# Attention: dividing the values' results instead of the probabilities, and moving the scores' scale and a sign onto the normalised queries

## The chip, the cores and the metric

The kernel runs on one core of one Trainium2 chip. The metric is the device time of one execution in microseconds (us), as the median of several runs; each version is also profiled once by the hardware profiler, and the rows in this document come from those profiles. PE is TensorE's matmul, PEld its weight load, DVE is VectorE, ACT is ScalarE, POOL is GpSimd and SP is SyncE.

## What is computed

The reference is a two-layer backbone of a diffusion generator: 512 latent tokens and 256 context tokens of width 1024. Each layer projects the normalised tokens into three groups of heads (attention, a state-space scan in both directions, and a Hyena long convolution), joins them in an output projection, and then applies a mixture of 16 experts. Only attention matters here:

```python
ql = apply_rope(rmsnorm(heads(q_l, ATT_HEADS), q_norm[i]), cos, sin)      # 6 query heads of 64
kl = apply_rope(rmsnorm(heads(k_l, ATT_KV_HEADS), k_norm[i]), cos, sin)   # 2 key and value heads
kc = rmsnorm(heads(k_c, ATT_KV_HEADS), k_norm[i])
att_l = gqa_blocks(ql, jnp.concatenate([kc, kl], axis=1), jnp.concatenate([vc, vl], axis=1))
att_c = gqa_blocks(qc, kc, vc)                 # in layer 0 only

def one_block(qi):                             # 128 queries at a time
    s = jnp.einsum('bqgrd,bkgd->bgrqk', qi, k).astype(jnp.float32) * scale    # scale = 1/8
    p = jax.nn.softmax(s, axis=-1).astype(v.dtype)
    return jnp.einsum('bgrqk,bkgd->bqgrd', p, v)
```

## The kernel before

Tokens lie in blocks of 128 (`P`): four latent blocks and two context blocks. Each layer first projects to queries, keys and values (`qkv`). `rotate` then normalises them: for each block it squares (L856) and sums (L857) each head's 64 values into `ss`, whose last axis holds six query heads and two key heads; L858 and L859 turn this into reciprocal roots, and L864 multiplies the heads by them. `to_heads` transposes queries and keys into `QT` and `KT`.

`attention` works through the six heads for one pair of query blocks at a time: blocks 0 and 1 against all six key blocks, blocks 2 and 3 against all six, and in layer 0 the two context blocks against the two context key blocks. That makes 18 calls of `values` in layer 0 and 12 in layer 1, and 60 calls of `scores`, one per head and query block. `scores` puts the products of a query block with all keys into a double PSUM bank of kind "A" (L920), takes the maximum over the keys (L923, VectorE) and multiplies it by -0.125 (L924, VectorE), takes the exponential on ScalarE with that as bias and 0.125 as scale, which also adds up the row's sum `su` (L927), and inverts the sum (L929, VectorE). GpSimd then multiplies the probabilities `pt` by it (L930). `values` runs one head later, so that the scores of the next head are under way. It goes through the key blocks two at a time, here called a round: TensorE transposes four 128x128 pieces of the probabilities into a PSUM bank (L939), VectorE or ScalarE copies them to `ph` (L942), and TensorE multiplies them with the values into the bank `po` (L945), the first query block on rows 0 to 63 and the second on rows 64 to 127. A call has three rounds for six key blocks and one round for two: 42 rounds in layer 0 and 36 in layer 1, 78 in all. Two ScalarE copies (L951) then bring the result into `mixa`.

Attention is a generator, and `weave` mixes its steps with other work. In layer 0 these are the last of the scan, then the Hyena convolutions (`hy_conv`, L517 on) and matmuls of the modulation (L256); in layer 1 projections, then scan (`ssd_states` and `ssd`, L670 on) and convolutions. The convolutions multiply spectra on VectorE (L551, L552, L554 to L556, L558) and on GpSimd (L550, L553, L557, L559); L540 adds a PSUM bank to an SBUF tile on VectorE. In the scan, GpSimd has L735, L740, L751, L774 and half of L717 and L718.

The order in which each engine gets its instructions is made ahead of time: the program is traced in the order of the code, and a scheduler with a simulated timeline (`schedule_with_timeline_sim=True`) places each instruction in its engine's queue. An engine then takes its queue in order. PSUM has eight banks; `B0` and `BA`, `B3` say how many each kind of use has. In layer 0's attention kind "A" has two double banks and kind "p" (`po` and the transposes) two banks. In layer 1, kind "A" has one double bank; "p" shares three banks with others (`BA`), and later has two of its own (`B3`).

## Time and profile before

| what | value |
|---|---|
| median of three runs | 1469.62 us (1465.35 to 1476.77) |
| the profiled execution: its time | 1466.34 us |
| the profiled execution: its span | 1464.4 us |
| mean granted TensorE clock | 0.925 of 2.4 GHz |
| instructions | 23682 |

The span is the time from the first to the last instruction; what lies around it is 1.9 us. A row of the trace that groups instructions gives the line of the code, the engine, the operation, the tile written and the tiles read, shapes and a count, then the busy time of the group, the mean duration of one in ns, and how long the engine stood idle just before them with what ended most of that. The granted clock is a share of full speed. It has two levels, 0.5 (1.2 GHz) and 1.0 (2.4 GHz), so 0.88 over a stretch says how long each was granted.

### The profile page before, as it was taken

What the parts mean: (1) busy time and instruction counts of PE and PEld (TensorE: products, weight loads), DVE (VectorE), ACT (ScalarE), POOL (GpSimd) and SP (SyncE); (2) the same over time, 40 slices, a digit from 0 to 9 for tenths busy, and PEclk for the clock granted to TensorE, in tenths of its full rate; (3) what the DMA queues carried; (4) which work ended last, traced back from release to release, by engine and by line L of the source; (5) the groups of instructions that cost most, each with busy time, mean ns of one, the idle gap of its engine ahead of it and who ended that gap; (6) DMA issues with size and microseconds to landing.
All of it is one profiled execution on the core that took longest, in us unless ns stands there. A gap on an engine that the chain in (4) does not pass through costs nothing. (4 is left out here: it accounts for less than half of the span.)

```text
span 1464.4 us, 23682 instructions
## 1 busy us (share of the span) xinstructions
PE 1248.4 (85%) x8904; PEld 899.8 (61%) x8904; DVE 760.8 (52%) x1661; ACT 488.4 (33%) x1056; POOL 453.9 (31%) x497
## 2 busy tenths in 40 slices
PE   5999999899899899869998949988988888599780
PEld 2787787677677677634544428876776776345440
DVE  6854652644667875852332334754498475512121
ACT  4332334445233453311110144444454542111111
POOL 3220321544334524222323311321188412222221
PEclk9999999997799999979998969999999899699995
DMA  7744536343655163279999551111301173999954
GB/s 295 241 157 158 173 102 215 118 152 132 206 161 184 58 244 117 86 275 369 340 322 279 110 173 44 58 58 44 138 30 58 41 288 129 352 371 353 354 115 137
DMA packets 88809, 265.04 MB, mean 181 GB/s; under 512 B 10397, under 2 KB 13101, under 8 KB 88048
## 3 DMA queue, kind: packets, MB, share of 16 engines
q1 hardware_dynamic: 76016, 224.39, 43.5%
q0 software_dynamic: 12672, 39.07, 10.4%
q8 instruction: 72, 1.18, 0.3%
q14 instruction: 49, 0.40, 0.1%
HBM read 231.62 MB, written 31.79 MB: 180 GB/s over the span
## 5 line engine op out<-in xcount | busy, mean ns | idle before, releaser
L1417 PE MATMUL bank<-we,xh 128*32 128x128 f32 (+3 forms) x1280 | 208.7, 394 | 12.1 <-DVE y L1473 8.6
L1417 PEld LDWEIGHTS bank<-we,xh 128*32 128x32 f32 (+3 forms) x1280 | 99.5, 139 | 106.1 <-issue 76.9
L219 PE MATMUL bank<-hh,hw 128*128 128x512 f32 (+1 forms) x440 | 159.5, 362 | 0.1
L220 PE MATMUL bank<-hl,hw 128*128 128x512 f32 (+1 forms) x440 | 157.1, 357 | 0.0
L221 PE MATMUL bank<-hh,lw 128*128 128x512 f32 (+1 forms) x440 | 156.7, 356 | 0.4 <-DVE lw L207 0.4
L1474 POOL DMA_INDIRECT xd<-y,txi x35 | 56.6, 1618 | 177.7 <-DMA xd<-y,txi 90.2
L1417 PE MATMUL bank<-we,gh 128*32 128x256 f32 (+3 forms) x392 | 101.0, 522 | 2.8 <-ACT gh L1450 1.4
L219 PEld LDWEIGHTS bank<-hh,hw 128*128 128x128 f32 x440 | 85.4, 194 | 12.1 <-issue 1.0
L221 PEld LDWEIGHTS bank<-hh,lw 128*128 128x128 f32 x440 | 84.6, 192 | 12.8 <-DVE lw L207 0.9
L220 PEld LDWEIGHTS bank<-hl,hw 128*128 128x128 f32 x440 | 85.0, 193 | 11.4 <-issue 0.8
L930 POOL TENSOR_SCALAR pt<-pt,su 128x768 f32<-128x768 f32 (+1 forms) x60 | 55.0, 924 | 118.6 <-DVE su L929 97.6
L256 PE MATMUL bank<-mraw,c 128*32 128x128 f32 x1536 | 72.8, 295 | 16.9 <-DMA mraw<-in_wm_dram 11.8
L1393 POOL DMA_INDIRECT xg<-hd,tk x40 | 40.4, 1009 | 96.6 <-PE bank L1407 32.7
L207 DVE TENSOR_TENSOR lw<-rw,hw 128x1024 fp32r<-128x1024 f32 (+1 forms) x36 | 44.7, 1243 | 49.1 <-ACT hw L206 48.9
L256 PEld LDWEIGHTS bank<-mraw,c 128*32 128x32 f32 x1536 | 41.2, 114 | 41.4 <-DMA mraw<-in_wm_dram 16.0
L945 PE MATMUL bank<-ph,vt 128*64 128x128 f32 x624 | 53.8, 292 | 15.1 <-DVE ph L942 7.0
L1417 PEld LDWEIGHTS bank<-we,gh 128*32 128x32 f32 (+3 forms) x392 | 35.7, 143 | 49.6 <-issue 41.8
L220 PE MATMUL bank<-lo,mh 128*128 128x512 f32 x160 | 63.8, 399 | 1.5 <-DVE lo L207 1.5
L219 PE MATMUL bank<-ho,mh 128*128 128x512 f32 x160 | 64.5, 405 | 0.4 <-ACT ho L206 0.4
L221 PE MATMUL bank<-ho,ml 128*128 128x512 f32 x160 | 63.2, 395 | 0.0
L206 ACT CAST hw<-rw 128x1024 fp32r<-128x1024 f32 (+1 forms) x36 | 37.8, 1049 | 76.1 <-PE bank L220 48.0
L923 DVE TENSOR_REDUCE mx<-banks 128x1 f32<-128x768 f32 (+1 forms) x60 | 50.3, 844 | 23.3 <-PE banks L920 23.1
(478 smaller groups left out, 2744.9 us busy)
## 6 DMA issues: line engine op xcount, KB each, us to landing
we<-in_we_dram SPq DMA_DIRECT2D x192, 512.0 KB, 11.3
mraw<-in_wm_dram SPq DMA_DIRECT2D x192, 256.0 KB, 3.6
rw<-in_wi_dram SPq DMA_DIRECT2D x34, 512.0 KB, 3.5
ro<-in_wo_dram SPq DMA_DIRECT2D x16, 512.0 KB, 4.9
G<-ar SPq DMA_DIRECT2D x10, 768.0 KB, 3.9
xd<-ox SPq DMA_DIRECT2D x10, 512.0 KB, 2.7
hd<-h POOLq DMA_DIRECT2D x10, 512.0 KB, 2.9
xf<-xd SPq DMA_DIRECT2D x10, 512.0 KB, 7.0
```

What stands on the lines that cost most here:

```text
L206: ACT.copy(hi, src)
L207: (lo_eng or DVE).tensor_sub(lo, src, f(hi))
L219: PE.matmul(o, lh, rh, start=start, stop=False)
L220: PE.matmul(o, lh, rl, start=False, stop=False)
L221: PE.matmul(o, ll, rh, start=False, stop=stop)
L256: PE.matmul(ps[32 * k:32 * k + 32, 0:P], c32[:, 4 * h + k, 30 - 2 * j:62 - 2 * j], raw[:, k], start=(j + h == 0), stop=(j == n - 1 and h = ...
L923: DVE.tensor_reduce(mx, ps, axis=AX.XY, op=OP.max)
L930: POOL.tensor_scalar(pt[:, 0:nkt * P], pt[:, 0:nkt * P], su, 1.0, OP.mult, OP.mult)
L945: PE.matmul(po[64 * q:64 * q + 64, 0:P], vt[:, k0 + kt + j, h // 3], ph[:, (2 * j + q) * P:(2 * j + q + 1) * P], start=(kt + j == 0), stop ...
L1393: POOL.indirect_dma_start(out=xg[0:c], out_offset=None, in_=hd, in_offset=bass.IndirectOffsetOnAxis(ap=R.token(i)[0:c], axis=0))
L1417: PE.matmul(ps[r:r + c, 0:m], lh[:, 0:c], w[:, m * j:m * j + m], start=start, stop=stop)
L1474: POOL.indirect_dma_start(out=xd.rearrange("t (n m) -> (t n) m", n=n), out_offset=bass.IndirectOffsetOnAxis(ap=R.row(i)[r], axis=0), in_=y ...
```

## The change

The queries' reciprocal roots are multiplied by -0.125 in `rotate`, so that a product of scores comes out as minus an eighth of what it was. The minimum over the keys is then the bias of the exponential as it stands, and the exponential's scale is -1. The probabilities stay undivided. `scores` returns the inverted sums beside them, and `su` has six buffers instead of four. In the first round of a call of `values`, two further matmuls, with the inverted sums repeated over 64 columns as the stationary operand and the identity as the moving one, spread the inverted sums of the two query blocks over the other 128 columns of the bank `po`, each over 64 rows. At the end ScalarE copies these columns to SBUF (`rb`, one copy of 128x128), and VectorE multiplies each half of the result by them while it brings it into `mixa`, in place of the two ScalarE copies.

```diff
@@ -857,6 +857,8 @@
             DVE.tensor_reduce(ss[:, t, h0:8], sq[:, h0:8], axis=AX.X, op=OP.add)
         ACT.activation(ss, ss, AF.Sqrt, bias=eps, scale=1.0 / HD)
         DVE.reciprocal(ss, ss)
+
+        DVE.tensor_scalar(ss[:, :, 0:6], ss[:, :, 0:6], -0.125, None, OP.mult)
         for t in range(TA):
             h0 = 0 if t < nq else 6
             nh = 8 - h0
@@ -920,15 +922,13 @@
                     PE.matmul(ps[:, j, 0:hw], QT[:, h, qs], KT[:, h // 3, x, ks], start=(x == 0), stop=(x == 1))
             ps = ps[:, 0:nb, 0:hw]
             mx = sm.tile([P, 1], F32, name="mx", bufs=4)
-            DVE.tensor_reduce(mx, ps, axis=AX.XY, op=OP.max)
-            DVE.tensor_scalar(mx, mx, -0.125, None, OP.mult)
+            DVE.tensor_reduce(mx, ps, axis=AX.XY, op=OP.min)
             pt = pool.tile([P, 768], F32, name="pt", bufs=PB[l])
-            su = sm.tile([P, 1], F32, name="su", bufs=4)
-            ACT.activation(pt[:, 0:nkt * P].rearrange("p (a b) -> p a b", a=nb), ps, AF.Exp, bias=mx, scale=0.125,
+            su = sm.tile([P, 1], F32, name="su", bufs=6)
+            ACT.activation(pt[:, 0:nkt * P].rearrange("p (a b) -> p a b", a=nb), ps, AF.Exp, bias=mx, scale=-1.0,
                            accum_out=su)
             DVE.reciprocal(su, su)
-            POOL.tensor_scalar(pt[:, 0:nkt * P], pt[:, 0:nkt * P], su, 1.0, OP.mult, OP.mult)
-            return pt
+            return pt, su
 
         def values(h, q0, k0, nkt, pts):
             po, busy["po"] = bank("p"), True
@@ -936,19 +936,27 @@
                 ps = bank("p")
                 for j in range(2):
                     for q in range(2):
-                        PE.transpose(ps[:, (2 * j + q) * P:(2 * j + q + 1) * P], pts[q][:, (kt + j) * P:(kt + j + 1) * P],
+                        PE.transpose(ps[:, (2 * j + q) * P:(2 * j + q + 1) * P], pts[q][0][:, (kt + j) * P:(kt + j + 1) * P],
                                      ident)
                 ph = pool.tile([P, 512], F32, name="ph", bufs=2)
                 (ACT.copy if kt % 4 else DVE.tensor_copy)(ph, ps)
+                if kt == 0:
+
+                    for q in range(2):
+                        PE.matmul(po[64 * q:64 * q + 64, P:2 * P], pts[q][1].to_broadcast([P, 64]), ident, start=True,
+                                  stop=True)
                 for j in range(2):
                     for q in range(2):
                         PE.matmul(po[64 * q:64 * q + 64, 0:P], vt[:, k0 + kt + j, h // 3],
                                   ph[:, (2 * j + q) * P:(2 * j + q + 1) * P], start=(kt + j == 0), stop=(kt + j == nkt - 1))
                 if kt == 2:
                     yield
+            rb = pool.tile([P, P], F32, name="rb", bufs=2)
+            ACT.copy(rb, po[:, P:2 * P])
             for q in range(2):
                 s = slice((q0 + q) * P, (q0 + q + 1) * P)
-                ACT.copy(mix[64 * (h % 2):64 * (h % 2) + 64, h // 2, s], po[64 * q:64 * q + 64, 0:P])
+                r = slice(64 * q, 64 * q + 64)
+                DVE.tensor_mul(mix[64 * (h % 2):64 * (h % 2) + 64, h // 2, s], po[r, 0:P], rb[r])
             busy["po"] = False
             yield
 
```

## Rows read from the trace of the kernel before

**Rows 1.** The page: each engine's busy time, share of the span, instructions.
```profile
PE 1248.4 (85%) x8904; PEld 899.8 (61%) x8904; DVE 760.8 (52%) x1661; ACT 488.4 (33%) x1056; POOL 453.9 (31%) x497
```

**Rows 2.** Busy time of each engine by stretch, the header naming the columns.
```profile
core 0: us, PE busy (x) PEld busy (x) DVE busy (x) ACT busy (x) POOL busy (x), PEclk, DMA share, GB/s
380.00:521.00 141.00, 129.10 (x1334) 101.06 (x1334) 105.89 (x248) 61.21 (x155) 63.61 (x72) 0.98 0.43 138
1000.00:1180.00 180.00, 159.17 (x1118) 127.22 (x1117) 117.45 (x226) 86.99 (x203) 86.37 (x88) 0.92 0.19 63
1065.00:1140.00 75.00, 63.69 (x472) 51.48 (x472) 66.13 (x118) 37.74 (x99) 61.26 (x56) 0.88 0.13 43
```

**Rows 3.** PE's waits, 380 to 550 us: waiter, releaser, total us, times, longest.
```profile
PE bank L945 <- ACT ph L942: 3.0, 5, 1.0
PE bank L945 <- DVE ph L942: 2.6, 5, 0.8
PE banks L920 <- ACT pt L927: 1.8, 4, 0.6
...
PE bank L945 <- ACT mh L998: 0.9, 1, 0.9
...
PE bank L939 <- POOL pt L930: 0.2, 1, 0.2
PE bank L945 <- DVE mx L924: 0.2, 1, 0.2
```

**Rows 4.** PE's waits, 1000 to 1180 us.
```profile
PE bank L945 <- DVE ph L942: 4.3, 5, 1.8
PE bank L945 <- DVE mx L924: 3.0, 5, 0.8
...
PE banks L920 <- ACT pt L927: 2.1, 4, 0.8
...
PE bank L939 <- POOL pt L930: 0.4, 2, 0.2
```

**Rows 5.** Groups with L930: whole span; then 1065 to 1140 us.
```profile
L930 POOL TENSOR_SCALAR pt<-pt,su 128x768 f32<-128x768 f32 (+1 forms) x60 | 55.0, 924 | 118.6 <-DVE su L929 97.6
...
L930 POOL TENSOR_SCALAR pt<-pt,su 128x768 f32<-128x768 f32 x10 | 11.5, 1150 | 5.3 <-DVE su L929 5.1
```

**Rows 6.** Groups of PE by form: the values' matmuls.
```profile
L945 PE MATMUL bank<-ph,vt 128*64 128x128 f32 x624 | 53.8, 292 | 15.1 <-DVE ph L942 7.0 <-ACT ph L942 3.9 <-DVE mx L924 3.2
```

**Rows 7.** Groups of VectorE by form, 380 to 550, then 1000 to 1180 us.
```profile
L924 DVE TENSOR_SCALAR mx<-mx 128x1 f32<-128x1 f32 x36 | 5.0, 146 | 0.3
L260 DVE COPY ms<-bank 128x128 f32<-128x128 f32 x7 | 2.0, 283 | 1.7 <-PE bank L256 1.7
...
L795 DVE SCALAR_TENSOR_TENSOR mixs<-mixs,vec,bank 64x128 f32<-64x128 f32 x8 | 2.7, 343 | 0.1
```

**Rows 8.** Timeline: from L924 to the exponential (start us, us, engine).
```profile
1153.15 0.15 DVE L924 TENSOR_SCALAR mx<-mx 128x1 f32<-128x1 f32 x1
1153.42 0.90 ACT L927 ACTIVATE pt<-banks,mx 128x768 f32<-128x768 f32 x1 [2.50 <-DVE mx L924]
```

**Rows 9.** VectorE by form: 380 to 550, then 1065 to 1140 us.
```profile
L540 DVE TENSOR_TENSOR Z<-bank,zo 128x256 f32<-128x256 f32 x12 | 5.1, 423 | 3.9 <-ACT zo L539 3.4
L551 DVE TENSOR_TENSOR t<-Z,Kt 128x512 f32<-128x512 f32 x6 | 4.1, 688 | 0.1
...
L551 DVE TENSOR_TENSOR t<-Z,Kt 128x512 f32<-128x512 f32 x3 | 3.5, 1160 | 0.0
L540 DVE TENSOR_TENSOR Z<-bank,zo 128x256 f32<-128x256 f32 x6 | 2.5, 415 | 0.0
```

**Rows 10.** L951 on ScalarE: its group to 550 us, then its waits in layer 1.
```profile
L951 ACT COPY mixa<-bank 64x128 f32<-64x128 f32 x36 | 9.4, 260 | 10.0 <-PE bank L945 9.6
...
ACT mixa L951 <- PE bank L945: 7.1, 5, 3.8
```

**Rows 11.** Timeline: the end of layer 1's attention.
```profile
1176.21 0.66 PE L945 MATMUL bank<-ph,vt 128*64 128x128 f32 x8 [0.17 <-DVE ph L942]
...
1176.91 0.53 ACT L951 COPY mixa<-bank 64x128 f32<-64x128 f32 x2 [3.77 <-PE bank L945]
```

## The prediction

> **What bounds the kernel now.** I read the page's line of busy shares first: PE is busy 85% of the span, VectorE 52%, ScalarE 33%, GpSimd 31% [rows 1]. The edits touch only attention, so the second view is the busy time by stretch [rows 2]. Attention runs twice, from about 380 to 521 us in layer 0, woven with the Hyena convolutions, and from about 1000 to 1180 us in layer 1, woven with projections, the scan and the convolutions. In the first stretch PE is busy 129.1 of 141 us at a granted clock of 0.98: PE is the bound, with 12 us of gaps. In the second it is busy 159.2 of 180 us at 0.92, and inside it 1065 to 1140 us differs: PE is busy 63.7 of 75 us at 0.88 while VectorE has 66.1 and GpSimd 61.3. There the two elementwise engines, not PE, set the pace.
>
> The third view says what PE's gaps end on [rows 3, 4]. Most stand in front of the values' matmuls (L945), which wait for the copy `ph` of the transposed probabilities; a few of those are put down to `mx` L924, a VectorE instruction that ends at the same moment as the copy. Together they are 6.7 us in 12 waits in layer 0 (3.0 + 2.6 + 0.9 + 0.2) and 7.3 us in 10 waits in layer 1. Scores (L920) wait for the exponential to free their PSUM bank: 1.8 and 2.1 us. For the multiplication that the change removes (L930) PE waited 0.2 and 0.4 us. So the 55.0 us that GpSimd spends on it [rows 5] are hidden from PE almost entirely; that is the main fact here.
>
> **The change part by part.** *TensorE, added.* `values` is called 30 times (18 in layer 0, 12 in layer 1), and each call gets two matmuls of the shape of L945. The trace has 624 records for 312 such matmuls in 53.8 us [rows 6], so 0.172 us each: 60 x 0.172 = 10.3 us. They stand between the copy `ph` and the matmuls that wait for it, but only in the first of a call's rounds: 30 of 78 rounds. If the 22 waits fall evenly, 22 x 30/78 = 8.5 are in such rounds, and each hides at most one pair (0.34 us): -2.9. Five of the calls fall into 1065 to 1140 us (10 of the 60 exponentials and multiplications are there [rows 5]), where PE is not the bound: I take another 1.2 off. Bounds: 0 (all in gaps) to +10.3. Taken: +6.2.
>
> *VectorE in the chain of scores, removed.* 60 times the small multiplication L924, 0.146 us [rows 7]. The exponential starts when it has ended [rows 8], and the exponential releases the bank that the next scores wait for. PE waited there 8 times; 8 x 0.15 = -1.2. `min` for `max` and the constants of the exponential change nothing in shape.
>
> *GpSimd, removed.* L930, 60 times, 55.0 us. Direct: -0.6 from PE's rows. Indirect: between 1065 and 1140 us ten of them take 11.5 us. The rows show that VectorE and GpSimd hinder each other there: VectorE's product L551 of two SBUF tiles takes 0.688 us on average in layer 0 and 1.160 us in this stretch, while L540, which reads PSUM, keeps 0.423 and 0.415 us [rows 9]. So taking GpSimd's work away also frees VectorE. The bounds are 0 (other GpSimd work moves up and collides instead) and -11.5 (the stretch shrinks by all of it). L930 is 11.5 of the 127.4 us that both engines are busy there, 9%, which on 75 us is 6.8; since VectorE gets work back, I take -4. The Trainium skill, "SBUF — State Buffer", section "SBUF: two separate sides", says that a VectorE instruction with two SBUF inputs and a GpSimd instruction hold one shared port pair exclusively, the loser blocking fully. The trace agrees in kind (1.160 against 0.688 us); if that rule alone set this stretch, the sum would take the far end, -11.5, instead of -4.
>
> *VectorE, added.* 60 products of 64x128 from PSUM. The nearest rows are the copy of 128x128 from PSUM, 0.283 us, and the three-operand product of 64x128, 0.343 us [rows 7]; I take 0.283, the simpler operation: 17.0 us. Against 60 x 0.146 = 8.8 removed, VectorE gets 8.2 us more. Where PE is the bound this lies beside PE's work; where VectorE is nearly full it delays `ph`, for which PE waits. Bounds 0 to +8.2; as VectorE is 75% busy in layer 0's stretch [rows 2], I take +1.5.
>
> *ScalarE.* Two copies of 0.26 us per call become one: -7.8 us on an engine that is 33% busy [rows 1, 10]. Nothing.
>
> *End of a call.* Today the last L945 is followed by two ScalarE copies, 0.53 us together [rows 11], and then by the casts of the output projection. Afterwards one copy (0.26) and two products on another engine (0.57) follow one another: about 0.3 us and a hand-over more, once at the end of each layer's attention: +0.8 in all. The Trainium skill, "PSUM — Partial Sum Buffer", section "PSUM bank collisions raise a hardware error", speaks against the change here: two engines may not touch one bank at once, so the copy of the sums, which lie in the bank of the results, may have to wait for the last L945. No row shows it; if the copy could run before, the +0.8 would be about +0.3.
>
> *The extra scaling in `rotate`.* One VectorE operation on 128x36 per layer, between 0.146 us (128x1) and 0.343 us (128 elements and three operands) [rows 7], in a chain that other work covers in part: +0.3 for both. The two more `su` buffers cost nothing: L939 and L945 are ordered behind the reciprocal already.
>
> Sum: 6.2 - 1.2 - 0.6 - 4.0 + 1.5 + 0.8 + 0.3 = +3.0 us on the profiled execution's 1466.3, so 1469.3. The median of the three runs shown, 1469.6, stands 3.3 above that execution, which gives 1472.6. I forecast the middle, 1471.
>
> **The rivals.** *PE pays the full price.* If the new matmuls fill no gaps and GpSimd's freed time returns nothing, what is left is 10.3 + 1.5 + 0.8 + 0.3 = +12.9: 1479.2, +0.9%. For it speaks PE's 92% in layer 0's stretch; against it the gaps in front of L945 just where the new matmuls stand.
>
> *VectorE and GpSimd are the bound of layer 1 (faster).* Then L930's 11.5 us go in full, and PE, with fewer gaps, is granted its upper level, 2.4 GHz, more often. Layer 1's attention has 159.2 us of PE work at 0.92; at 1.00 that is 12.7 less. 1466.3 + 6.2 - 1.2 - 0.6 + 1.5 + 0.8 + 0.3 - 11.5 = 1461.8 without the clock, 1449.1 with all of it; about 1452 at its likeliest. For it speaks GpSimd's 61.3 of 75 us and the stretched products; against it that VectorE is fuller still and keeps its load, and that GpSimd waited for the reciprocals in front of L930 (97.6 us over the span [rows 5]) and not the other way round. The rule of the Trainium skill on the shared port pair ("SBUF — State Buffer", as above) would make this rival the outcome.
>
> *VectorE waits where ScalarE waited (slower).* The divisions need the last L945. Today ScalarE stood idle for that 9.6 us in layer 0 and 7.1 in 5 waits in layer 1 [rows 10]; the divisions put this wait into VectorE's queue, with the next reductions and `ph` copies behind it, for both of which PE waits. If all of it reaches PE: 1469.3 + 16.7 = 1486.0. It decides from about 12 us of the 16.7 on. For it speaks that VectorE is 88% busy from 1065 to 1140 us; against it that PE has other woven work to go on with.
>
> *The order changes.* The order of instructions on each engine is made ahead of time by a simulated timeline; other durations can shift it everywhere. I know no sign and widen the range by some us.
>
> **How the numbers follow.** My forecast, +3.0 or nearly so, 0.50; PE pays in full 0.20; faster 0.17; slower 0.13. About 1% is what a measurement of this kernel can tell from no change; the three runs alone span 11 us. Within 1% lie the first two, less their far edges: 0.68. Faster by over 1%: 0.16. Slower: 0.16, the third rival and the edge of the first. The range reaches into both outer cases, 1453 to 1484; the forecast's own is 1464 to 1477.
>
> **What would show it.** In the profile after: L930 gone and GpSimd near 399 us; 60 more logical matmuls, near 0.17 us each, behind the first `ph` of a call; divisions of about 0.28 us on VectorE, with idle time in front of them released by L945 (under 5 us for my forecast, over 12 for the slow rival); PE's busy time 10 us higher. Between 1065 and 1140 us, VectorE's two-SBUF products near 0.69 us and a granted clock over 0.95 would prove the fast rival. The forecast is wrong if PE's busy time does not rise, or if its waits for `ph` change by more than 5 us.

## The result and the profile after

The changed kernel takes 1485.74 us (median of four runs, 1484.36 to 1489.61), the kernel before beside it 1468.34 us: a ratio of 1.0132, 95% interval 1.0097 to 1.0167. It is 17.4 us slower, 1.3%. I had forecast 1471 with a range to 1484. In all medians and ratios of this document one run of e3 (1827 us), one of e16 (4398 us) and one of the kernel before beside e9 to e12 (1533 us) are left out, because they stand far outside the others. The profiled execution of after took 1484.52 us, its span is 1482.3 us and its clock 0.926.

In the code of after, line numbers move: L924 is gone and the minimum is L925, the exponential L928, the reciprocal L930 (the old L930, GpSimd's division, is gone), the transposes stay L939, the added matmuls are L946, the values' matmuls L950 (before L945), the copy of the sums L955, and the divisions L959.

The page's line of busy times, which answers [rows 1]:

```profile
PE 1257.2 (85%) x9024; PEld 903.7 (61%) x9024; DVE 771.4 (52%) x1663; ACT 479.6 (32%) x1026; POOL 400.0 (27%) x437
```

GpSimd lost 53.9 us and PE gained 8.8, as the change says. The work is where it should be, yet the time went up by twice what PE gained in busy time. The windows of the stretches that answer [rows 2], shifted to about the same work (start:end, length, then busy us and records of PE, PEld, DVE, ACT, POOL, the granted clock, DMA share, GB/s):

```profile
386.00:527.00 141.00, 129.71 (x1352) 99.88 (x1353) 104.94 (x230) 51.76 (x124) 34.12 (x36) 0.98 0.42 131
1012.00:1192.00 180.00, 152.59 (x1098) 122.54 (x1096) 119.54 (x218) 78.95 (x179) 65.16 (x67) 0.93 0.17 60
1078.00:1153.00 75.00, 60.15 (x486) 48.91 (x485) 69.80 (x118) 36.72 (x94) 50.34 (x46) 0.93 0.13 43
```

Layer 0's stretch is as full of PE as before. In layer 1 PE does less in the same 180 us (152.6 against 159.2), so its work is done later. In the inner 75 us, where I had hoped that VectorE would become freer, GpSimd fell from 61.3 to 50.3 us and VectorE rose from 66.1 to 69.8.

The waits of PE after, first in 386 to 556 us of layer 0, then in 976 to 1204 us of layer 1 (waiter, releaser, total us, times, longest):

```profile
PE bank L256 <- DMA mraw<-in_wm_dram: 3.6, 5, 1.7
...
PE bank L939 <- DVE mixa L959: 2.6, 1, 2.6
PE bank L950 <- DVE ph L942: 1.8, 6, 0.7
PE bank L950 <- ACT ph L942: 1.8, 3, 0.7
```

```profile
PE bank L480 <- DVE ud L475: 6.6, 3, 3.3
PE bank L946 <- DVE ph L942: 4.8, 1, 4.8
PE bank L701 <- DVE xw L696: 4.7, 3, 2.7
PE bank L950 <- ACT ph L942: 3.5, 3, 2.6
PE bank L939 <- DVE mixa L959: 3.1, 1, 3.1
PE banks L922 <- ACT pt L928: 2.5, 3, 2.0
PE bank L950 <- DVE ph L942: 2.5, 5, 0.8
PE bank L946 <- DVE mixa L959: 2.1, 2, 1.8
```

And of before in layer 1 (964 to 1185 us) the rows of two waits that are not in [rows 4]:

```profile
PE bank L701 <- DVE xw L696: 2.8, 4, 1.4
...
PE bank L480 <- DVE mx L924: 2.8, 1, 2.8
```

One kind of wait is new and belongs to the change: PE waits for the divisions (L959) that free the bank of results, 2.6 us in layer 0 and 3.1 + 2.1 in layer 1. Another grew, and the change does not touch its lines: L480, transposes of the Hyena input, waits 6.6 us for VectorE's L475, where the row of before has 2.8 us, put down to L924. One wait of 2.8 us stands in both (at 979.5 us before, at 991.8 after); what is new is one of 0.5 us and one of 3.3 us. The timelines show where the 3.3 us come from, before, then after:

```profile
1013.00 0.97 PE L920 MATMUL banks<-KT,QT 128*128 128x384 f32 x4
...
1014.48 1.09 PE L939 MATMUL bank<-cst,pt 128*128 128x128 f32 x8
...
1018.13 0.74 PE L480 MATMUL bank<-cst,ud 128*128 128x128 f32 x4
```

```profile
1025.78 1.09 PE L950 MATMUL bank<-ph,vt 128*64 128x128 f32 x16
1030.21 1.10 PE L480 MATMUL bank<-cst,ud 128*128 128x128 f32 x4 [3.34 <-DVE ud L475]
```

Before, PE's queue has scores, transposes and values between the last projection matmul and this L480, so PE works while VectorE prepares its input. After, only a few matmuls of the values stand there, and PE waits. The order in PE's queue is what changed here.

In layer 0 the longest wait of after has nothing to do with the new instructions: L256 waits 3.6 us for its weights by DMA, where it waited 0.7 us before.

The costs of the new instructions, by form over the whole span:

```profile
L959 DVE TENSOR_TENSOR mixa<-bank,rb 64x128 f32<-64x128 f32 x60 | 17.2, 287 | 9.3 <-ACT rb L955 8.6
L946 PE MATMUL bank<-cst,su 128*64 128x128 f32 x120 | 14.8, 311 | 8.3 <-DVE ph L942 5.5 <-DVE mixa L959 2.1 <-ACT pt L928 0.3
```

The divisions took 17.2 us (17.0 forecast). The 60 added matmuls took 14.8 us, 0.247 each, not the 0.172 that I had worked out from [rows 6].

### The profile page after: what moved, and what is told of

It is laid out like the page before. It is cut to its first block, busy times and chain, and to the rows that moved or that the text cites. A ratio compares the mean times of both kernels' runs of the same rounds, so it can differ in the third digit from the quotient of the medians.

```text
span 1482.3 us, 23830 instructions
## 1 busy us (share of the span) xinstructions
PE 1257.2 (85%) x9024; PEld 903.7 (61%) x9024; DVE 771.4 (52%) x1663; ACT 479.6 (32%) x1026; POOL 400.0 (27%) x437
## 3 DMA queue, kind: packets, MB, share of 16 engines
q0 software_dynamic: 12672, 39.07, 10.3%
## 5 line engine op out<-in xcount | busy, mean ns | idle before, releaser
L219 PE MATMUL bank<-hh,hw 128*128 128x512 f32 (+1 forms) x440 | 160.6, 365 | 0.1
L221 PE MATMUL bank<-hh,lw 128*128 128x512 f32 (+1 forms) x440 | 157.8, 359 | 0.4 <-DVE lw L207 0.4
L219 PEld LDWEIGHTS bank<-hh,hw 128*128 128x128 f32 x440 | 86.1, 196 | 12.2 <-issue 1.0
L221 PEld LDWEIGHTS bank<-hh,lw 128*128 128x128 f32 x440 | 85.5, 194 | 13.0 <-DVE lw L207 0.9
L220 PEld LDWEIGHTS bank<-hl,hw 128*128 128x128 f32 x440 | 85.7, 195 | 11.7 <-issue 0.8
L256 PE MATMUL bank<-mraw,c 128*32 128x128 f32 x1536 | 73.0, 295 | 19.3 <-DMA mraw<-in_wm_dram 15.0
L256 PEld LDWEIGHTS bank<-mraw,c 128*32 128x32 f32 x1536 | 40.3, 114 | 45.4 <-DMA mraw<-in_wm_dram 21.8
L928 ACT ACTIVATE pt<-banks,mx 128x768 f32<-128x768 f32 (+1 forms) x60 | 48.6, 813 | 50.8 <-DVE mx L925 35.6
L950 PE MATMUL bank<-ph,vt 128*64 128x128 f32 x624 | 55.8, 301 | 9.7 <-ACT ph L942 5.3
L219 PE MATMUL bank<-ho,mh 128*128 128x512 f32 x160 | 63.4, 400 | 0.0
L221 PE MATMUL bank<-ho,ml 128*128 128x512 f32 x160 | 62.7, 392 | 0.0
L939 PE MATMUL bank<-cst,pt 128*128 128x128 f32 x312 | 54.6, 298 | 6.0 <-DVE mixa L959 5.7
```

The lines of the kernel that those rows point to most:

```text
L219: PE.matmul(o, lh, rh, start=start, stop=False)
L220: PE.matmul(o, lh, rl, start=False, stop=False)
L221: PE.matmul(o, ll, rh, start=False, stop=stop)
L256: PE.matmul(ps[32 * k:32 * k + 32, 0:P], c32[:, 4 * h + k, 30 - 2 * j:62 - 2 * j], raw[:, k], start=(j + h == 0), stop=(j == n - 1 and h = ...
L928: ACT.activation(pt[:, 0:nkt * P].rearrange("p (a b) -> p a b", a=nb), ps, AF.Exp, bias=mx, scale=-1.0, accum_out=su)
L939: PE.transpose(ps[:, (2 * j + q) * P:(2 * j + q + 1) * P], pts[q][0][:, (kt + j) * P:(kt + j + 1) * P], ident)
```

## The experiments

The table shows every kernel that was timed. Ratios are against the kernel before, run beside it. The last two columns come from one profiled execution each and are differences to the kernel before: "layer 0" from the first scores (L920) to the router (L1240), 251.4 us before, and "layer 1" from its first scores to the first L221 of the output projection, 220.7 us before. The four rows marked "same work" change practically no work. I compared the order in which PE ran its records, by line and shape, with that of before: of the 8904 records, the fewest that must be moved to make the two agree are 2 in e11, 11 in e12, 7 in e8 and 155 in e15. In the change they are 534 (its 120 new records not counted), in e3 523. So where e8, e11 and e12 differ from before in these columns, by up to 3.3 and 5.6 us, it is the noise of one profile. The stretch of layer 1 does not hold the same work in every kernel: in e2, e3 and e7 the first scores stand 15 projection matmuls (L219 to L221) earlier in PE's queue than before, in e17 nine earlier, in e12 eight later. Counted from the same matmul on, these five stand at -1.5, +11.9, +3.1, +1.9 and -3.7 us; the others move by 0.3 or less.

| kernel | median us | ratio, 95% | layer 0 | layer 1 |
|---|---|---|---|---|
| the change | 1485.7 | 1.0132, 1.0097 to 1.0167 | +7.0 | +7.6 |
| e1 scale half | 1470.0 | 1.0025, 1.0004 to 1.0045 | -2.8 | +3.6 |
| e2 division half | 1479.0 | 1.0073, 1.0044 to 1.0101 | +4.7 | +1.4 |
| e3 no division | 1481.0 | 1.0086, 1.0052 to 1.0121 | -2.7 | +14.8 |
| e4 matmuls added | 1474.3 | 1.0042, 1.0020 to 1.0064 | +5.4 | -1.2 |
| e5 GpSimd divides results | 1483.8 | 1.0113, 1.0089 to 1.0136 | +10.4 | +2.7 |
| e6 change, 1.5 turns | 1485.5 | 1.0119, 1.0073 to 1.0166 | +7.4 | +10.4 |
| e7 no division, 1.5 turns | 1468.8 | 1.0008, 0.9990 to 1.0026 | -2.4 | +6.0 |
| e8 before, 1.5 turns (same work) | 1468.8 | 1.0022, 1.0004 to 1.0040 | +3.3 | -1.2 |
| e9 change, no spread | 1479.7 | 1.0102, 1.0060 to 1.0143 | +2.6 | +11.2 |
| e10 change, spread twice | 1478.8 | 1.0098, 1.0076 to 1.0120 | +8.2 | +0.3 |
| e11 null once (same work) | 1465.9 | 0.9998, 0.9970 to 1.0025 | +3.1 | -0.3 |
| e12 null twice (same work) | 1467.3 | 1.0014, 0.9997 to 1.0030 | +0.2 | -5.6 |
| e13 change, 3 turns | 1479.8 | 1.0079, 1.0050 to 1.0108 | +11.7 | +3.7 |
| e14 change, convolutions 1 turn | 1481.8 | 1.0092, 1.0057 to 1.0128 | +8.1 | +2.0 |
| e15 before, convolutions 0.4 (same work) | 1468.0 | 1.0009, 0.9982 to 1.0037 | +0.6 | +1.6 |
| e16 one spread matmul, 2 turns | 1484.6 | 1.0110, 1.0089 to 1.0132 | +8.0 | +5.5 |
| e17 change, L924 back | 1482.5 | 1.0109, 1.0066 to 1.0152 | +4.3 | +4.1 |
| e18 change, GpSimd's product back | 1484.4 | 1.0131, 1.0086 to 1.0175 | +11.4 | +5.1 |

### The two halves: e1 and e2

e1 does the queries' scale and sign alone, e2 the rest.

```diff
+        DVE.tensor_scalar(ss[:, :, 0:6], ss[:, :, 0:6], -0.125, None, OP.mult)
-            DVE.tensor_reduce(mx, ps, axis=AX.XY, op=OP.max)
-            DVE.tensor_scalar(mx, mx, -0.125, None, OP.mult)
+            DVE.tensor_reduce(mx, ps, axis=AX.XY, op=OP.min)
...  (left out: the scale of the exponential becomes -1.0)
```

> Only the half of the change on the queries: scale and sign move to the queries' norms, the reduction is a minimum, the small VectorE multiplication L924 is gone; GpSimd still divides the probabilities. Theories for the whole change's +17 us. Bring-out theory (the divisions on VectorE wait for a copy on ScalarE and hold the PSUM bank of the results, so that PE waits): this half is innocent, 0 to -2 us against before. PE-price theory (60 added matmuls where PE is the bound): the same, 0 to -2 us. Order theory (any edit makes the planner order all queues anew, and the new order is by chance worse): a shift of several us of either sign here too, 4 us or more.

> Only the other half: the values' results are divided, with the two added matmuls, the copy rb and the divisions on VectorE, while the scale, the maximum and L924 stay as before. Bring-out and PE-price theories: all of the loss is here, +14 to +20 us against before. Order theory: not bound to this half; anywhere from -5 to +20 us, and the two halves do not add up to the whole.

e1 gained nothing that can be measured by what it removed (+0.25%, as far from before as e8, which runs practically the same order), and e2 lost 0.73%, some 11 us, where both theories that put the whole loss there had 14 to 20. The sum of the halves is about 14 us, the whole 17.4: most of the loss is in the division half.

### The removal alone: e3, and with other turns: e7, e8, e6

e3 only deletes GpSimd's L930. e7 does the same and gives the attention 1.5 turns instead of 1 for each step of the scan in layer 1's last `weave`; e8 gives the kernel before these turns, e6 the changed kernel.

```diff
-            POOL.tensor_scalar(pt[:, 0:nkt * P], pt[:, 0:nkt * P], su, 1.0, OP.mult, OP.mult)
```

> The kernel before without GpSimd's multiplication L930 and with nothing in its place: the division by the softmax's sum is left out. It gives what the removal alone is worth. Bring-out and PE-price theories: GpSimd's freed 55 us return a little, 0 to -6 us. The rival that VectorE and GpSimd are the bound of layer 1: -8 to -15 us. Order theory: can even be slower than before, by some us.

> The kernel before without L930 (the division by the softmax's sum is left out), which took 1481.9 us, with DW 1.5 as in the run beside it. It has no added matmul and no division, so neither the PE price nor the bring-out can act. Order theory: its +14 us over before lie in layer 1's late attention and go with the earlier turns: 1462 to 1472 us. If it stays over 1478, its loss has another cause.

> The kernel before with DW 1.5, to see what the number does by itself. Order theory: its attention tail is shorter already (about 10 us), so the gain is smaller, 0 to -6 us against before, or a loss if the scan now ends last. The other theories say nothing of it.

> The changed kernel with one number changed: in layer 1's last weave attention gets 1.5 steps for each step of the scan instead of 1 (DW). Order theory, in its form for layer 1 (attention ends last there, in a chain of its own after scan and convolutions have ended, about 20 us of the changed kernel against 10 before): the tail shortens and the time falls by 5 to 12 us from 1485.7. Bring-out theory: less than 3 us of difference, since each call of values keeps its waits. PE-price theory: no difference.

e3 and e7 are the most telling pair of the study. e3 does less work than the kernel before and adds none, and it is 12.6 us slower (0.86%). With 1.5 turns instead of 1 the same instructions lose nothing (+0.08%), and the two intervals do not overlap. The orders of PE in the two differ in 148 of 8904 records. For the kernel before (+0.22%) and for the change (1485.5 against 1485.7, where 5 to 12 us less had been expected) the same turns do nothing, but they move less there: 7 and 60 records, and in e6 six rounds of the values still stand behind the last scan matmul, as in the change. The windows of layer 1's stretch, before first (from its first scores, then from the matmul that stands where e3's stretch begins), then e3:

```profile
963.90:1184.60 220.70, 192.65 (x1272) 154.19 (x1270) 137.97 (x262) 105.12 (x233) 90.86 (x95) 0.91 0.20 70
...
960.98:1184.60 223.62, 195.57 (x1288) 156.70 (x1287) 140.00 (x264) 106.73 (x236) 92.03 (x97) 0.92 0.20 69
```

```profile
963.20:1198.74 235.54, 198.11 (x1288) 158.36 (x1286) 141.35 (x263) 107.85 (x235) 68.62 (x72) 0.90 0.18 61
```

With the same 1288 records of PE, e3's stretch is 11.9 us longer. PE's idle time in it (length less busy) is 37.4 us against 28.1, and its busy time 2.5 us higher. VectorE has 1.4 us more busy time, although GpSimd has 23.4 us less. So taking 55 us from GpSimd bought nothing, and the new order of the queues cost something.

### The added matmuls alone: e4

The kernel before, division and all, with the 60 spread matmuls added and not read.

> The kernel before with the 60 added matmuls alone, whose result nobody reads; GpSimd still divides the probabilities and ScalarE brings the results out. PE-price theory: +8 to +12 us against before, most of the loss. Bring-out theory: +3 to +6 us, as gaps in front of the values' matmuls take part of it. Order theory: either sign.

+0.42%, 6.2 us (2.9 to 9.4), between what the two theories had expected (8 to 12 and 3 to 6). Of the two attention stretches, only layer 0's is longer. The windows from first scores to router, before first, then e4:

```profile
380.30:631.70 251.40, 226.23 (x1914) 180.60 (x1914) 186.12 (x453) 100.66 (x221) 94.17 (x95) 0.95 0.41 138
```

```profile
385.50:642.30 256.80, 232.64 (x1987) 183.72 (x1986) 186.43 (x454) 100.87 (x221) 92.84 (x95) 0.96 0.40 135
```

PE is busy 6.4 us longer and the stretch is 5.4 us longer. In layer 1 the same kernel is 1.2 us shorter than before. The whole table agrees: the eleven kernels with spread matmuls stand at +4.3 to +11.7 in layer 0 (mean +7.9), the others and the kernel before at -2.8 to +3.3 (mean +0.2).

### The bring-out off VectorE: e5

ScalarE copies the whole bank to SBUF once, and GpSimd multiplies there.

```diff
...  (left out: `rb` becomes 128x256)
-            ACT.copy(rb, po[:, P:2 * P])
+            ACT.copy(rb, po[:, 0:2 * P])
...
-                DVE.tensor_mul(mix[64 * (h % 2):64 * (h % 2) + 64, h // 2, s], po[r, 0:P], rb[r])
+                POOL.tensor_mul(mix[64 * (h % 2):64 * (h % 2) + 64, h // 2, s], rb[r, 0:P], rb[r, P:2 * P])
```

> The changed kernel with another way out of PSUM: one ScalarE copy brings result and spread sums (128x256) to SBUF and so frees the bank, and GpSimd, which has time since L930 is gone, does the two divisions from SBUF. VectorE has no divisions. Bring-out theory: PE's new waits for the divisions (5.7 us in front of L939, 2.1 us in front of L946) go, and VectorE gets back 17 us of work: 1472 to 1477 us, 8 us or more below the changed kernel's 1485.7. PE-price theory alone: no difference from the changed kernel (1483 to 1488). Order theory: anywhere between 1470 and 1490, with the late end of layer 1's attention still there.

1483.8 against 1485.7: with no division on VectorE and no wait for one, most of the loss stays. Layer 1's stretch is 4.9 us shorter than in the change, layer 0's 3.4 us longer. The divisions in VectorE's queue thus explain about 2 us of the whole; the intervals (1.0089 to 1.0136 against 1.0097 to 1.0167) leave room for a few more.

### Without the spread, and with it twice: e9 and e10

e9 deletes the spread matmuls and `rb` and brings the undivided results out with VectorE copies; e10 issues each pair twice.

```diff
-                    for q in range(2):
+                    for q in (0, 1, 0, 1):
```

> The changed kernel without the 60 spread matmuls, their bank half's copy on ScalarE and the division itself: VectorE brings the values' results out undivided, 60 copies in place of 60 products. Theory A (TensorE pays for the spread matmuls where it is the bound): layer 0, from the first scores to the router, loses the 5 to 7 us that it gained in every run with the added matmuls and stands 2 to 3 us below the kernel before; the whole is 1471 to 1477. Theory B (the bring-out on VectorE holds the values' bank): nothing changes there, since VectorE still brings out; the whole stays at 1482 to 1487. Theory C (the planner's new order of the queues makes the attention of layer 1 end late): layer 0 falls as in A, and layer 1's attention, from its first scores to the output projection's first matmul, stays 5 us or more over the kernel before: 1476 to 1482.

> The changed kernel with each pair of spread matmuls issued twice: 60 more of them. Theory A (the price of TensorE's added matmuls): 0.34 us more a call in the 18 calls of layer 0, some 6 us there, and 0 to 4 us more in layer 1's 12: 1490 to 1496 in all. If TensorE has room where they stand: 1484 to 1488. Theory C adds that layer 1 can move by 10 us either way with the order that the planner makes of it, so that layer 0 alone is the test.

e9 comes out mostly as theory C said: the whole lies in its range and layer 1 is 11.2 us over before. Layer 0 falls by 4.4 us, as the price of the matmuls wants, but stands 2.6 us above before and not 2 to 3 below. Theory B's range (from 1482) begins 2.3 us above the median, inside the interval; against it speaks that no wait for the bring-out stands among PE's rows in layer 1. What stands there are waits for the copies `ph`, which were 4.3 and 0.9 us in the kernel before (L945, released by L942), and 3.0 us put down to L924:

```profile
PE bank L945 <- ACT ph L942: 9.4, 7, 3.3
PE bank L945 <- DVE ph L942: 8.8, 11, 2.7
```

e10 misses every theory: it does more work than the change and is not slower. Its median is 7 us lower, its ratio 0.34% (5 us), and the intervals overlap. Layer 0 rises by 1.2 us where some 6 were expected; layer 1 falls by 7.3. The second pair is cheap: layer 0's 72 records of L946 take 8.6 us in the change, and these 144 in e10:

```profile
L946 PE MATMUL bank<-cst,su 128*64 128x128 f32 x144 | 12.7, 293 | 1.4 <-DVE ph L942 0.8 <-ACT pt L928 0.3 <-DVE mixa L959 0.2
```

### Does any edit cost? e11 and e12

The kernel before, with one or two products by 1.0 on the normalisers in each layer.

```diff
         DVE.reciprocal(ss, ss)
+        DVE.tensor_scalar(ss[:, :, 0:6], ss[:, :, 0:6], 1.0, None, OP.mult)
```

> The kernel before with one product by 1.0 on the normalisers in each layer, two small VectorE instructions of some 0.1 us in all. Theory C (any edit makes the planner order all queues anew, and the order before was a good one of many): 1470 to 1478, the difference in layer 1's attention or in front of the first scores. If the order is worth nothing: 1467 to 1469.

> The same with two such products in each layer, 0.2 us more: a second draw of an order. Theory C: 1470 to 1478, not in step with the number of products. If the order is worth nothing: 1467 to 1469, as with one.

These two do not: 0.9998 and 1.0014. But neither do they move the order. Beside a few VectorE instructions (PE's wait at L480 is 0.5 us in e12 instead of 2.8) both run in the order of before, and so does e8. So my theory that any edit makes all queues anew fell here, and what a new order costs is not tested by them. Of the kernels that keep every instruction, only e15 (155 records of PE in another place, +0.09%) and e4 (271 beside its own, layer 1 at -1.2) have a new order, and neither loses more by it in layer 1 than the noise.

### Rounds left over at the end of layer 1: e13, e14 and e15

In the kernel before, three rounds of the values stand in PE's queue behind the last matmul of the scan (L767); in the change six. The timelines (start us, duration, engine), before, then after:

```profile
1165.74 0.39 PE L767 MATMUL bank<-G,xtok 128*64 128x128 f32 x4
1168.29 0.66 PE L939 MATMUL bank<-cst,pt 128*128 128x128 f32 x4
1171.41 1.11 PE L939 MATMUL bank<-cst,pt 128*128 128x128 f32 x4
1173.89 0.66 PE L939 MATMUL bank<-cst,pt 128*128 128x128 f32 x4
```

```profile
1174.83 0.42 PE L767 MATMUL bank<-G,xtok 128*64 128x128 f32 x4
1175.61 0.44 PE L939 MATMUL bank<-cst,pt 128*128 128x128 f32 x2
1178.49 0.38 PE L939 MATMUL bank<-cst,pt 128*128 128x128 f32 x2
1182.37 1.12 PE L939 MATMUL bank<-cst,pt 128*128 128x128 f32 x4
1185.32 1.12 PE L939 MATMUL bank<-cst,pt 128*128 128x128 f32 x4
1187.81 0.66 PE L939 MATMUL bank<-cst,pt 128*128 128x128 f32 x4
1191.97 1.12 PE L939 MATMUL bank<-cst,pt 128*128 128x128 f32 x4
1194.81 1.12 PE L939 MATMUL bank<-cst,pt 128*128 128x128 f32 x4
```

After the scan the attention runs nearly alone: a round takes some 3 us, and most transposes run at the lower clock, 1.2 GHz (1.12 us for four against 0.66; the granted clock from 1182.3 to 1183.5 us is 0.50). e13 and e14 keep the change and bring the count to 2 and 3 by turns of the `weave` alone, 3 for the attention or 1 for the convolutions; e15 keeps the kernel before and raises it to 5.

```diff
-DW = 1
+DW = 3
```

> The changed kernel with 3 turns instead of 1 for the attention in layer 1's last weave. In TensorE's queue 2 rounds of the values stand behind the last scan matmul, where the changed kernel has 6. If the rounds left over are the cause of layer 1's part: from layer 1's first scores to its output projection 221 us or less (228.3 in the changed kernel, 220.7 before), the whole 1475 to 1480, with the matmuls' price in layer 0 left. If they are a companion only: 226 us or more there, 1483 to 1488.

> The changed kernel with 1 turn instead of 0.5 for the convolutions in that weave, another order with the same sign: 3 rounds behind the last scan matmul. Cause: 221 us or less in layer 1's stretch and 1475 to 1480; companion: 226 us or more and 1483 to 1488.

> The kernel before, division and all, with 0.4 instead of 0.5 turns for the convolutions in that weave: 5 rounds of the values behind the last scan matmul in place of 3. Cause: 3 to 8 us more in layer 1's stretch, 1470 to 1475. Companion: as before, 1466 to 1469.

The answer lies between. e13 and e14 are 5.9 and 4.0 us faster than the change by their medians, and layer 1's stretch is 3.9 and 5.6 us shorter, but neither comes down to 221 us; the intervals overlap with that of the change. e15 takes 1468.0 us, as if the count were a companion only. And e7 has eight rounds left over and is as fast as the kernel before. e18, below, has three rounds left over, as before the change, and its time is no lower than the change's. The rounds left over are at most a part of the loss.

### Half the matmuls: e16

One matmul of 128 columns a call instead of two of 64; GpSimd first widens the pair of inverted sums. The attention gets 2 turns, which leaves 2 rounds over.

```diff
...  (left out: the turns, and GpSimd's copy of the inverted sums to `sw`, 128x128)
-                    for q in range(2):
-                        PE.matmul(po[64 * q:64 * q + 64, P:2 * P], pts[q][1].to_broadcast([P, 64]), ident, start=True,
-                                  stop=True)
+                    PE.matmul(po[:, P:2 * P], sw, ident, start=True, stop=True)
```

> The changed kernel with one spread matmul of 128 columns a call instead of two of 64 (GpSimd widens the pair of sums to 128 columns first), and 2 turns for the attention: 2 rounds behind the last scan matmul. If half the matmuls cost half: 3 us less in layer 0 than the changed kernel; with the rounds as the cause of layer 1's part 1471 to 1477; without it 1480 to 1484.

It was meant as a better version and is none: 1484.6. Its 18 matmuls in layer 0 cost nearly what the change's 36 cost there (7.9 us against 8.6; its L945 is the added matmul), so layer 0 stays at +8.0:

```profile
L945 PE MATMUL bank<-cst,sw 128*128 128x128 f32 x36 | 7.9, 302 | 1.4 <-DVE ph L943 1.0 <-DVE mixa L957 0.3
```

### Removed instructions put back: e17 and e18

The change with a product by 1.0 in the place of one removed instruction: L924 in e17, GpSimd's L930 in e18.

```diff
+            DVE.tensor_scalar(mx, mx, 1.0, None, OP.mult)
```

```diff
+            POOL.tensor_scalar(pt[:, 0:nkt * P], pt[:, 0:nkt * P], 1.0, 1.0, OP.mult, OP.mult)
```

> The changed kernel with a product of the minimum by 1.0 in place of the removed L924: 60 VectorE instructions of 0.15 us more, on the path to the exponential. By their work alone: 0 to 3 us more than the changed kernel, 1485 to 1489. If the removal costs through the order: TensorE's wait for the copies of the Hyena input in layer 1 (L480, released by L475) goes back from 6.6 us to 2.8 as before, 4 rounds instead of 6 stand behind the last scan matmul, and the whole falls to 1476 to 1483.

> The changed kernel with GpSimd's product of the probabilities back, by 1.0 instead of the inverse sum: some 55 us of GpSimd's time and its step between exponential and transposes return, while VectorE still divides. By the work alone, with the 4 us of collisions that were forecast as a gain: 1485 to 1492. If the removal costs through the order: 3 rounds instead of 6 behind the last scan matmul, layer 1's attention 3 to 7 us shorter, the L480 wait still 6.6 us, and the whole 1476 to 1482.

e17, with 60 VectorE instructions more on the path to the exponential, is not slower than the change: its median is 3.3 us lower, with intervals that overlap. The wait that nobody had edited is back at its old size:

```profile
PE bank L480 <- DVE mx L926: 2.8, 1, 2.8
```

The kernels with the scale half and without that product (e1, e5, e6, e9, e10, e13, e14, e16, e18) all show 5.5 to 6.6 us there, the rest at most 3.1. So this wait goes with the removal of L924. What it costs is not shown: e10 has the full 6.6 us, and its layer 1 stands at +0.3.

e18 separates GpSimd's work from all else. The two stretches of after, then of e18:

```profile
385.60:644.00 258.40, 231.27 (x1986) 182.59 (x1986) 191.16 (x453) 94.14 (x202) 63.37 (x59) 0.96 0.40 134
976.10:1204.43 228.34, 193.93 (x1320) 155.63 (x1318) 143.90 (x261) 100.41 (x219) 66.92 (x71) 0.92 0.19 66
```

```profile
382.50:645.30 262.80, 235.28 (x1986) 185.12 (x1986) 195.03 (x453) 93.91 (x202) 90.32 (x95) 0.95 0.39 132
976.10:1201.87 225.77, 193.24 (x1320) 154.49 (x1318) 145.76 (x261) 101.86 (x221) 88.06 (x95) 0.92 0.20 69
```

In layer 1 GpSimd has 21.1 us back, VectorE 1.9 us more, and the stretch is 2.6 us shorter; in layer 0 it is 4.4 us longer, and 4.0 of these are busy time of PE on the same 1986 records, not idle time. The rounds left over fall from six to three, as had been expected if the removal costs through the order. The whole took 1484.4 us against 1485.7. So some 55 us of GpSimd's work [rows 5], in or out of the changed kernel, are worth nothing that can be measured. The recovery to 1476 to 1482 that belonged to this did not come: in the changed kernel putting GpSimd's step back does not bring the time back.

## Why the prediction was wrong

The main fact that I named, that GpSimd's 55 us are hidden from PE, was right, and I did not follow it: I still took 4 us for it. With the two gains of the sum that did not come (4.6 us for GpSimd, 1.2 us for L924) at nothing, it would have been +8.8 and not +3.0; the other 8.6 of the measured 17.4 us have no term in it, and most of what the runs say of them points at the order of the queues, which I had put at nothing. Point by point:

**The added matmuls, +6.2: the sum right, its terms not.** e4 measures +6.2 (2.9 to 9.4), so the agreement to the tenth is luck, and the 10.3 of the rival in which PE pays the full price lies just outside. But a spread matmul takes 0.247 us where I had 0.172, the price shows in layer 0, where PE is the bound, and nothing is visible in layer 1 (-1.2). I had priced a matmul by a row whose matmuls come four in a group, eight records [rows 11]; the spread pair stands alone. My discount for gaps was about as large as this mistake.

**GpSimd freed, -4.0 and -0.6: failed, measured 0.** This is the largest term of the sum that was wrong. The reading behind it, that the two elementwise engines and not PE set the pace from 1065 to 1140 us, did not hold: with GpSimd 10.9 us less busy in after's 75 us, PE was not fuller (60.2 us against 63.7). Removed alone (e3, e7), L930 gave +12.6 us and nothing; put back into the change (e18), it cost nothing. In after's inner stretch the products that were to become short did so only in part (VectorE by form, 1078 to 1153 us; the row of before, 1065 to 1140 us, follows):

```profile
L751 DVE TENSOR_TENSOR ce<-ctok,ea 128x192 f32<-128x192 f32 x8 | 6.1, 800 | 0.1
L555 DVE TENSOR_TENSOR t<-t,Z 128x512 f32<-128x512 f32 x4 | 4.9, 1234 | 0.1
...
L551 DVE TENSOR_TENSOR t<-Z,Kt 128x512 f32<-128x512 f32 x3 | 2.5, 850 | 0.0
L540 DVE TENSOR_TENSOR Z<-bank,zo 128x256 f32<-128x256 f32 x6 | 2.5, 412 | 0.0
```

```profile
L751 DVE TENSOR_TENSOR ce<-ctok,ea 128x192 f32<-128x192 f32 x8 | 4.5, 606 | 0.2 <-POOL H L718 0.2
...
L555 DVE TENSOR_TENSOR t<-t,Z 128x512 f32<-128x512 f32 x4 | 4.1, 1014 | 0.0
```

L551 fell from 1160 ns [rows 9] to 850, but L751 rose from 606 to 800 and L555 from 1014 to 1234, while L540, which reads PSUM, stayed at 412. L751 is split between VectorE and GpSimd, as L717 and L718 are. L555's eight records in the two stretches show the collision: the three with no GpSimd instruction beside them took 0.68, 0.68 and 0.69 us, the five others 0.91 to 2.10. VectorE and GpSimd still collide; only other pairs do. That was the zero end of my bounds, "other GpSimd work moves up and collides instead", and e18 agrees: its 48.1 us of GpSimd time (27.0 and 21.1 us in the two stretches) cost VectorE 5.7 us of busy time (3.9 and 1.9), and the time is the same. The Trainium skill, "SBUF — State Buffer", section "SBUF: two separate sides", says that a VectorE instruction with two SBUF inputs and a GpSimd instruction that reads SBUF take one shared port pair exclusively, and that the one that comes second waits. The long products agree with it in kind. What it would make of the stretch if it alone set it, 11.5 us less, did not come, and with it the fast rival falls. That rival's step from fewer gaps to a higher clock is not borne out either: in the 75 us PE was less busy after the change and the clock higher (0.93 against 0.88).

**L924 removed, -1.2: not measurable.** The scale half alone (e1) is 2.5 us slower than before, and putting a product back in its place (e17) did not make the change slower; both differences are of the size of the noise. The 0.15 us on the path are real, but a wait of 3.3 us and one of 0.5 at L480 came with the new order.

**VectorE's divisions, +1.5, and the slow rival.** The divisions' idle time was to tell: under 5 us for my forecast, over 12 for the rival. It was 8.6, between the two and released by the copy of the sums (L955), and the waits for the divisions in PE's rows are 7.8 us (2.6 + 3.1 + 2.1). e5, without any of them, gains 1.9 us. So +1.5 is not contradicted, and the rival's 1486.0 is close to the result mostly by chance: without its mechanism the time is 1483.8. The copy of the sums does wait for the last values' matmul, as I feared:

```profile
ACT rb L955 <- PE bank L950: 28.7, 18, 5.3
```

The Trainium skill, "PSUM — Partial Sum Buffer", section "PSUM bank collisions raise a hardware error", forbids two engines at the same partitions of one bank at once; the row shows the wait, and no run separates the chip's part in it from the program's own ordering of a bank's users.

**The order of the queues: the step that failed.** I wrote "I know no sign and widen the range by some us", and put the term at nothing. In the change, layer 1's stretch grew by 7.6 us while its PE work hardly changed; what grew is PE's idle time (34.4 us against 28.1). The table shows a sign. In the fourteen kernels that take an instruction from scores to results out or replace one, layer 1, counted from the same matmul on, stands at -1.5 to +11.9 us, mean +4.9, and only e2 is below zero. All fourteen have a new order, with 426 to 585 of PE's records in another place. In the two kernels that have a new order without that, e4 and e15 (271 and 155 records), it stands at -1.2 and +1.6. For the change itself layer 0 and layer 1 give 7.0 + 7.6 = 14.6 of the 17.4 us. The rest is not assigned: the profile of after is 5.3 us behind before already at its first scores, but e11, which differs there by one tiny product, is 6.6 us behind in its profile and not slower in its median.

My signs of being wrong did not look at this. PE's busy time rose by 8.8 us, as forecast, and its waits for `ph` hardly changed: 6.7 us before in layer 0 (0.9 of them, put down to `mh`, I had counted in) and 8.2 in layer 1, against 4.4 and 10.8 after.

Shown: order alone can cost this much. e3 and e7 have the same instructions in another order and lie 11 us apart by their ratios. Not shown: which piece of the new order costs the change its 7.6 us in layer 1. The wait at L480 is there in full in e10, which loses nothing in layer 1; three rounds left over do not help e18, and eight do not hurt e7; the change with other turns (e13, e14) is 4 to 6 us faster by its medians, with intervals that overlap. The waits for the divisions are 5.2 us of layer 1's idle time in after, and e5, which has none, is 4.9 us shorter there, but only 1.9 us in the whole. Not settled either: why the orders after a removal or a replacement are mostly worse. e4 and e15 speak against a new order as such, but they are two and move fewer records; e1 and e7 move 453 and 518, and the whole kernel is only 0.25% and 0.08% slower; e18 shows that putting GpSimd's step back is not enough; and e3's 12.6 us, which vanish with other turns, show that it can come with removed work alone. The scheduler works with a simulated timeline, and a natural guess is that its order fits the old chain by chance or by tuning of the turns; that is argued, not shown. No kernel here beats the one before: its closest rivals, e11 and e12, are practically the same kernel.

## What to carry to other kernels

When the engine that bounds a stretch waits 0.4 us for 55 us of another engine's work, plan with 0.4 us for its removal and not with what it might loosen: here it gave nothing that could be measured. Where queues are ordered ahead of time by a simulated timeline, an edit has two prices, its instructions and the order that follows. A null edit tells what order alone costs only if it moves the order, so compare the queues first: three of the four here hardly moved it. An edit that only removes work (e3), run with other turns beside it (e7), tells whether the second price is there. Before two stretches are compared, check that they hold the same work: the first scores of e3 stand 15 matmuls earlier, which made its loss look 2.9 us larger. Price a small matmul by a row where it stands as alone as it will stand.

## What the runs showed of the hardware

A pair of spread matmuls of 64 columns cost 0.478 us a call in layer 0 (8.6 us over 18 calls), one of 128 columns 0.44 (7.9 over 18), and two pairs 0.706 (12.7 over 18). The second pair added 0.228 us, about half of what the first costs.

The end of layer 1's attention, a chain through PE, the copies and PE again, ran at a lower granted clock in after, where more of it stands alone. The windows of its last stretch, before and after:

```profile
1160.00:1185.00 25.00, 21.37 (x175) 17.99 (x172) 16.87 (x41) 13.47 (x26) 4.16 (x10) 0.87 0.36 132
```

```profile
1172.00:1204.00 32.00, 27.77 (x197) 22.50 (x195) 17.78 (x45) 12.09 (x24) 2.01 (x7) 0.72 0.21 79
```

At 0.72, more than half of after's last 32 us were granted 1.2 GHz. In the inner 75 us ahead of them the clock was higher than in the kernel before (0.93 against 0.88), and over the whole of layer 1's stretch it was 0.92 against 0.91. So the low clock at the end is not what makes the stretch longer; PE's idle time is.
